# An MLP made of seven products: its operands' sums taken product by product, its weights' sums moved to VectorE, and its products in another order

## The chip, the cores and the metric

The kernel runs on one core of a Trainium2 chip. The metric is the device time of one execution in microseconds (us). Before the change it is 1749.95 us, the median of three runs (1748.13 to 1752.63). Engines are named as in the profile: PE is TensorE, DVE VectorE, ACT ScalarE, POOL GpSimd and SP SyncE.

## The reference

An encoder of two layers goes over 768 tokens (512 of one batch, 256 of the other) with 1024 features. Layer 0 mixes neighbourhood and grouped-query attention, layer 1 is differential attention. Behind each attention stands an MLP, which is what the change touches:

```python
h = rmsnorm(x, ln_mlp[layer])
x = x + jnp.square(jax.nn.relu(h @ w_up[layer])) @ w_down[layer]   # 1024 -> 4096 -> 1024
```

After layer 1 comes a last RMSNorm. Everything is in float32.

## The kernel before

**Products.** Activations stay transposed: features on the 128 partitions, tokens along the row. Each float32 operand is split into a high part, which ACT writes (whi, th, c), and the rest, which DVE subtracts (wlo, and the second half of th and c); a product is then three matmuls: high by high, high by low, low by high. In the MLP both matrix products are cut into 2 by 2 blocks (the tokens into halves A and B of 384) and made of seven block products instead of eight, so there are sums of blocks to make before the products and sums of products after them.

**The up projection** goes over 16 slices of 256 hidden features (mp). `weights()` makes four sums of weight blocks on POOL (L839) and splits them. The sums of activation blocks are made once per layer. `first()` splits the four plain blocks (c 0 to 3) while the output projection of the attention is still running. `second()` makes the other four (c 4 to 7): for each of four feature rows j it makes one scaled copy on ACT (L803) and four sums on DVE (L790), and splits four results with `put` (ACT and DVE, L116 and L117). The first slice is made of the eight plain products, which need c 0 to 3 only; `second()` runs beside it. The second slice takes its products in the order 1, 3, 2, 6, 4, 7, 5, so c 6 is the first sum that PE needs. The tile t of `second()` has three buffers, shared with z, in which a slice's results stand. `finish` (L873 on) writes a slice's squared results and their sums to DRAM, in seven slots: three by a DMA on ACT's queue straight from z, four by two DMAs on POOL's queue after more DVE sums.

**The down projection** has 28 steps: seven products n, each over four quarters i of the hidden features. A step is 48 matmuls (four output blocks r, four slices q, three parts). Before it, `operand` loads the slot from DRAM (tr, L915, SP's queue) and splits it (th); `fetch` loads two weight tiles (L986, SP's queue, three steps ahead); `sums` adds them on POOL to the tile kept from the product before (L993, for products 5, 6, 3 and 7, two per step); `halves` splits the sum (L80, L81). In the loop the order is: fetch of step s+3, sums and operand of s+2, halves of s+1, then the matmuls of s (L1034). At the end of a product its four PSUM banks are folded into the accumulators e, f and h or into x (L862, L1007); products 1 and 7 end with a longer run of such operations.

Tile sets the semaphores and the order on each engine, starting from the order of the program. What the PE is to do next waits in order; a DVE instruction that waits holds up the ones behind it, and so does a DMA in SP's queue.

Of the kernel before, what the change touches and what calls it, by code (L numbers as in the profile page):

```python
# [11 lines left out]
F32 = mybir.dt.float32  # L12
F32R = mybir.dt.float32r
AF = mybir.ActivationFunctionType
ALU = mybir.AluOpType
# [22 lines left out]
def kernel(ctx: ExitStack, tc: tile.TileContext, a: dict, y: bass.AP):  # L38
# [90 lines left out]
    def gcol(g, k):  # L129
        return gains[:, g, k : k + 1]  # L130
# [643 lines left out]
    def mlp(layer, src, o, x, es):  # L774
# [10 lines left out]
        def put(pool, c, j, src, gain=None):  # L785
            t = comb[c, j] = pool.tile([P, 2, HT], F32R, tag=f"c{c}", name=f"c{c}", bufs=4)
            halve(t[:, 0], t[:, 1], src, gain)

        def stt(out, x_, s, y_, op):
            nc.vector.scalar_tensor_tensor(out=out, in0=x_, scalar=s, in1=y_, op0=ALU.mult, op1=op)  # L790
# [5 lines left out]

        def second():

            ts = []
            for j in range(4):  # L800
                xa, xb = x[j], x[j + 4]
                t = up.tile([P, 4, HT], F32, tag="z", name="t", bufs=3)
                nc.scalar.activation(t[:, 0], xa[:, A], AF.Copy, scale=gcol(g, j))  # L803
                stt(t[:, 1], xa[:, B], gcol(g, j), t[:, 0], ALU.subtract)
                stt(t[:, 2], xb[:, A], gcol(5 + layer, j + 4), t[:, 1], ALU.subtract)
                put(g2, 6, j, t[:, 2])
                stt(t[:, 3], xb[:, B], gcol(g, j + 4), t[:, 2], ALU.add)
                put(g2, 4, j, t[:, 3])
                stt(t[:, 0], xb[:, A], gcol(g, j + 4), t[:, 0], ALU.subtract)
                put(g2, 7, j, t[:, 0])  # L810
                put(g2, 5, j, t[:, 1])

        run(out_proj(src, o, None, x, 1, first))
        es.close()
# [46 lines left out]
        def add(out, x_, y_, op=ALU.add):  # L861
            nc.vector.tensor_tensor(out=out, in0=x_, in1=y_, op=op)  # L862
# [49 lines left out]
        def operand(n, i):  # L912

            tr = pa_.tile([P, ND, HT], F32, tag="tr", name="tr", bufs=2)
            nc.sync.dma_start(tr, T[i][:, SLOT[n]])  # L915
            th = pa_.tile([P, 2, ND, HT], F32R, tag="th", name="th", bufs=3)
            halve(th[:, 0], th[:, 1], tr)
            return th

        for mp in range(first_mp, FF // 256):  # L920
            w = weights() if mp > first_mp else w2
            one = lambda n: product(bank(n), w[n], n)
            p1 = one(1)
            z = ztile()
            z12, z11, z22, z21 = z[:, 0, A], z[:, 0, B], z[:, 1, A], z[:, 1, B]
            nc.scalar.activation(z11, p1, AF.Copy)
            p3, p2 = one(3), one(2)
            if mp == FF // 256 - 1:

                g1s.close()  # L930
                pa_ = g1s.enter_context(tc.tile_pool(name=f"dna{layer}", bufs=4, reuse_waits="tile"))
                ths = [operand(4, 0)]
            add(z12, one(6), z11)
            add(z11, p2, z11)
            if wait:
                finish(wait.pop(0))
            p4 = one(4)
            add(z22, one(7), z12)
            add(z21, p4, z22, ALU.subtract)
            add(z12, p3, z12)  # L940
            if wait:
                finish(wait.pop(0))
            p5 = one(5)
            nc.vector.scalar_tensor_tensor(out=z22, in0=p5, scalar=-1.0, in1=z22, op0=ALU.mult, op1=ALU.subtract)
            add(z12, p5, z12)
            square(z)
            finish(z)
            if 4 <= mp < 4 + KD:
                nm.add(x[MO[mp - 4]])
            elif mp == 4 + KD:  # L950
                rt = nm.rstd()
# [10 lines left out]
        wds = ExitStack()  # L962
        ch = wds.enter_context(tc.tile_pool(name="ch", bufs=8, side="right", reuse_waits="tile"))
        wd = wds.enter_context(tc.tile_pool(name="wd", bufs=6, side="right", reuse_waits="tile"))
        e, f, h = (acs.tile([P, 4, HT], F32, name=f"{n}_{layer}") for n in "efh")
        PR = (0, 1)
        ORDER = (4, 5, 6, 3, 1, 7, 2)

        BLOCK = {1: 11, 2: 12, 7: 21, 4: 22, 5: 21, 6: 11, 3: 12}
        steps = [(n, i) for n in ORDER for i in range(NG)]  # L970
# [3 lines left out]
        def fetch(n, i):  # L974

            for rp in PR:
                off = (((layer * NG + i) * 4 + (11, 22, 21, 12).index(BLOCK[n])) * 2 + rp) * P * 1024
                if n in (1, 4) and (n, i) != (4, 0):
                    t = ch.tile([P, 1024], F32, tag="ch", name="ch", bufs=8)
                else:  # L980
                    third[0] += n != 4
                    if n == 4 or third[0] % 3 == 0:
                        t = wpool.tile([P, 1024], F32, tag="wraw", name="wd", bufs=3)
                    else:
                        t = wd.tile([P, 1024], F32, tag="wd", name="wd", bufs=6)
                nc.sync.dma_start(t, a["w_down"][off : off + P * 1024].rearrange("(p w) -> p w", w=1024))  # L986
                (kept if n in (1, 4) else new)[i, rp] = t

        def sums(n, i):
            for rp in PR:  # L990
                if n in (7, 5, 6, 3):
                    t = kept[i, rp]
                    nc.gpsimd.tensor_tensor(out=t, in0=t, in1=new.pop((i, rp)), op=ALU.add)  # L993

        def halves(n, i):
            for rp in PR:
                hi, lo = whilo(1024)
                wsplit(hi, lo, new.pop((i, rp)) if n == 2 else kept[i, rp])
                parts[n, i, rp] = hi, lo

        def fold(out, x_, op=ALU.add):
            add(out, out, x_, op)
# [4 lines left out]
            nc.vector.tensor_tensor(out=out, in0=x_, in1=rr, op=ALU.mult)  # L1007

        xb = lambda r, i, sl: x[2 * r + i][:, sl]
        for s in range(3):  # L1010
            fetch(*steps[s])
        halves(*steps[0])
# [2 lines left out]
        for s, (n, i) in enumerate(steps):  # L1015
            if s + 3 < len(steps):
                fetch(*steps[s + 3])
            if s + 2 < len(steps):
                sums(*steps[s + 2])
                ths.append(operand(*steps[s + 2]))  # L1020
            if s + 1 < len(steps):
                halves(*steps[s + 1])
            if i == 0:
                odd = ORDER.index(n) % 2
                banks = [ps_tile("at" if odd or r == 3 else "mm", "dn")[:, :HT] for r in range(4)]
            th = ths.pop(0)

            for passes in (((0, 0), (1, 0)), ((0, 1),)) if s == 0 else (((0, 0), (0, 1), (1, 0)),):
                for r, ps in enumerate(banks):
                    w = parts[n, i, r // 2]  # L1030
                    for q in range(ND):
                        c = (r % 2) * 512 + q * P
                        for a_, b_ in passes:
                            nc.tensor.matmul(ps, w[a_][:, c : c + P], th[:, b_, q], start=i + q + a_ + b_ == 0,  # L1034
                                             stop=i == NG - 1 and q == ND - 1 and a_ == 1)
            if i == NG - 1:
                for r, ps in enumerate(banks):
                    if n == 4:
                        nc.scalar.activation(f[:, r], ps, AF.Copy)
                    if n == 5:  # L1040
                        nc.scalar.activation(h[:, r], ps, AF.Copy)
                    if n == 3:
                        add(e[:, r], ps, h[:, r])
                    if n in (6, 1, 7):
                        fold(f[:, r], ps, ALU.subtract)
                        fold(h[:, r], ps)
                    if n == 1:
                        fold(e[:, r], ps)
                    if n in (1, 2):
                        t = acs.tile([P, HT], F32, tag="t", name="t", bufs=4)  # L1050
                        scaled(t, ps, B)
                        fold(xb(r, 0, B), t)
                if n == 1:
                    scaled(e, e, A)
                    for r in range(4):
                        fold(xb(r, 0, A), e[:, r])
                if n == 7:
                    scaled(h, h, A)
                    for r in range(4):
                        fold(xb(r, 1, A), h[:, r], ALU.subtract)  # L1060
                    scaled(f, f, B)
                    for r in range(4):
                        fold(xb(r, 1, B), f[:, r])
            if layer == 1 and n == 2 and i < NG - 1:
                last[0](i)
            elif layer == 1 and n == 7 and i == NG - 1:
                tiles = iter([(e, r) for r in range(4)] * 4)

                def sq():
                    e_, r = next(tiles)  # L1070
                    return e_[:, r]

                last = [final(x, sq, s_, R2[:, A]) for s_ in (0, HT)]
        if layer == 1:
# [208 lines left out]
```

## Time and profile before

| | |
|---|---|
| median of three runs | 1749.95 us |
| the profiled execution: its time | 1750.86 us |
| its span | 1749.1 us |
| PE busy | 1708.8 us (98%) |
| DVE busy | 1356.3 us (78%) |
| ACT busy | 874.0 us (50%) |
| POOL busy | 568.7 us (33%) |

The profile is one execution. A busy PE means that a matmul was in it, at whatever clock was granted. In a timeline the number in square brackets is the idle time of the engine just before the instruction, and after the arrow stands what ended it. A matmul of the MLP is 128x384 and starts every 175 ns when nothing holds it up.

### The profile page before, as it was taken

The page shows a single profiled execution, that of the slowest core. Times are in us where ns is not written, and L with a number is a line of the kernel's source. Part 1 is how long each engine was busy: PE and PEld are TensorE (multiplying, and loading weights), DVE is VectorE, ACT ScalarE, POOL GpSimd, SP SyncE. Part 2 cuts the span into 40 slices and gives each one's busy share as a digit, 9 for nine tenths or more (in the row PEclk, how much of TensorE's full clock was granted, in tenths as well). Part 3 has the DMA queues.
Part 4 walks back from the last instruction along what each step waited for, and adds up shares of the span by engine and source line. Part 5 has one row for each costly group of instructions (what it writes and reads, how often), then busy time and mean ns, then how long its engine had stood idle before and what let it go on. Part 6 is the DMA issues. An engine that isn't in the chain of part 4 may idle for free. (4 is left out here: it accounts for less than half of the span.)

```text
span 1749.1 us, 28353 instructions
## 1 busy us (share of the span) xinstructions
PE 1708.8 (98%) x10964; PEld 1623.4 (93%) x10964; DVE 1356.3 (78%) x2214; ACT 874.0 (50%) x1553; POOL 568.7 (33%) x443
## 2 busy tenths in 40 slices
PE   8999999999999999999999999999999999999997
PEld 7888888889999999999999999988899999899997
DVE  7888647499777699888676776776898776899885
ACT  6765434365444453444435555554555444544442
POOL 2200000025555288340021222210346553693501
PEclk9999999999999999999999999999999999999998
DMA  4111222414544687853410110122145546868521
GB/s 170 37 46 49 69 77 91 136 47 147 178 165 156 224 300 258 301 163 133 130 53 25 49 49 22 55 64 92 48 154 170 167 167 198 293 241 326 188 73 72
DMA packets 74597, 235.42 MB, mean 135 GB/s; under 512 B 7904, under 2 KB 25056, under 8 KB 74464
## 3 DMA queue, kind: packets, MB, share of 16 engines
q1 hardware_dynamic: 52480, 186.93, 32.1%
q0 software_dynamic: 7168, 25.17, 4.0%
q10 hardware_dynamic: 14816, 21.52, 3.4%
q8 instruction: 86, 1.41, 0.3%
q14 instruction: 47, 0.39, 0.1%
HBM read 182.47 MB, written 50.33 MB: 133 GB/s over the span
## 5 line engine op out<-in xcount | busy, mean ns | idle before, releaser
L854 PE MATMUL up<-c,whi 128*128 128x384 f32 x1808 | 463.8, 338 | 5.4 <-ACT c L116 4.3
L1034 PE MATMUL dn<-th,whi 128*128 128x384 f32 x1792 | 461.6, 339 | 3.7 <-DVE th L117 3.7
L854 PEld LDWEIGHTS up<-c,whi 128*128 128x128 f32 x1808 | 328.1, 188 | 7.4 <-ACT c L116 5.0
L1034 PEld LDWEIGHTS dn<-th,whi 128*128 128x128 f32 x1792 | 326.6, 188 | 4.6 <-DVE th L117 4.2
L1034 PE MATMUL dn<-th,wlo 128*128 128x384 f32 x896 | 302.9, 339 | 5.9 <-DVE wlo L81 5.9
L854 PE MATMUL up<-c,wlo 128*128 128x384 f32 x904 | 304.1, 338 | 0.5 <-DVE wlo L81 0.5
L839 POOL TENSOR_TENSOR s<-wraw 128x512 f32<-128x512 f32 x60 | 92.8, 1553 | 412.5 <-PE npv L601 258.9
L993 POOL TENSOR_TENSOR ch<-ch,wd 128x1024 f32<-128x1024 f32 x52 | 174.7, 3375 | 86.3 <-DVE wlo L81 76.0
L81 DVE TENSOR_TENSOR wlo<-ch,whi 128x1024 fp32r<-128x1024 f32 x80 | 157.8, 1998 | 27.0 <-ACT whi L80 26.8
L1034 PEld LDWEIGHTS dn<-th,wlo 128*128 128x128 f32 x896 | 168.7, 188 | 7.5 <-DVE wlo L81 7.5
L854 PEld LDWEIGHTS up<-c,wlo 128*128 128x128 f32 x904 | 170.2, 188 | 1.2 <-DVE wlo L81 1.2
L80 ACT ACTIVATE whi<-wraw 128x1024 fp32r<-128x1024 f32 (+3 forms) x128 | 116.3, 910 | 92.8 <-PE up L854 57.0
L81 DVE TENSOR_TENSOR wlo<-wraw,whi 128x1024 fp32r<-128x1024 f32 (+3 forms) x132 | 145.6, 1103 | 17.4 <-ACT whi L80 16.7
L80 ACT ACTIVATE whi<-ch 128x1024 fp32r<-128x1024 f32 x80 | 84.6, 1062 | 132.7 <-PE dn L1034 94.2
L117 DVE TENSOR_TENSOR th<-tr,th 128x1536 fp32r<-128x1536 f32 x56 | 143.7, 2566 | 5.8 <-ACT th L116 5.6
L80 ACT ACTIVATE whi<-s 128x1024 fp32r<-128x1024 f32 x60 | 63.8, 1064 | 118.6 <-PE up L854 106.8
L196 PE MATMUL dqk<-whi,xh 128*128 128x256 f32 x384 | 114.7, 299 | 0.0
L81 DVE TENSOR_TENSOR wlo<-s,whi 128x1024 fp32r<-128x1024 f32 x60 | 83.4, 1390 | 35.3 <-ACT whi L80 35.2
L116 ACT ACTIVATE th<-tr 128x1536 fp32r<-128x1536 f32 x56 | 83.0, 1482 | 49.6 <-DMA tr<-T 45.3
L196 PE MATMUL dqk<-whi,xl 128*128 128x256 f32 x384 | 107.5, 280 | 0.0
L196 PE MATMUL dqk<-wlo,xh 128*128 128x256 f32 x384 | 107.2, 279 | 0.0
L706 ACT ACTIVATE de<-ds,m 128x512 f32<-128x512 f32 (+1 forms) x96 | 58.3, 612 | 81.6 <-DVE m L704 81.6
(231 smaller groups left out, 3773.4 us busy)
## 6 DMA issues: line engine op xcount, KB each, us to landing
wd<-in_w_down_dram SPq DMA_DIRECT2D x84, 512.0 KB, 5.2
tr<-T SPq DMA_DIRECT2D x56, 768.0 KB, 5.2
wraw<-in_w_up_dram SPq DMA_DIRECT2D x64, 512.0 KB, 3.7
T<-t POOLq DMA_DIRECT2D x64, 384.0 KB, 3.2
T<-z ACTq DMA_DIRECT2D x32, 576.0 KB, 3.0
ch<-in_w_down_dram SPq DMA_DIRECT2D x28, 512.0 KB, 6.1
wraw<-in_w_in_o_dram SPq DMA_DIRECT2D x24, 512.0 KB, 3.6
wraw<-in_w_in_e_dram SPq DMA_DIRECT2D x16, 512.0 KB, 3.7
```

The lines of the kernel that those rows point to most:

```text
L80: nc.scalar.activation(hi, raw, AF.Copy)
L81: nc.vector.tensor_tensor(out=lo, in0=raw, in1=hi.bitcast(F32), op=ALU.subtract)
L116: nc.scalar.activation(hi, src, AF.Copy)
L117: nc.vector.tensor_tensor(out=lo, in0=src, in1=hi.bitcast(F32), op=ALU.subtract)
L196: nc.tensor.matmul(ps[:, :256], st[:, tk], col(k, part, 0, 256), start=(k == 0 and i == 0), stop=(k == KD - 1 and i == 2))
L706: nc.scalar.activation(e, s, AF.Exp, bias=m, scale=1.0, accum_out=l2[:, c : c + 1])
L839: nc.gpsimd.tensor_tensor(out=d_, in0=x_, in1=y_, op=ALU.add)
L854: nc.tensor.matmul(ps, part[a_][:, base + k * P : base + (k + 1) * P], t[:, b_], start=start and k + i == 0, stop=stop and k == 3 and i == 2)
L993: nc.gpsimd.tensor_tensor(out=t, in0=t, in1=new.pop((i, rp)), op=ALU.add)
L1034: nc.tensor.matmul(ps, w[a_][:, c : c + P], th[:, b_, q], start=i + q + a_ + b_ == 0, stop=i == NG - 1 and q == ND - 1 and a_ == 1)
```

## The change

`second()` gets room for all four rows at once (two z buffers, the ninth x tile, and the tile R) and goes over the rows once per product: c 6 of all rows, then c 4, then c 7, then c 5. In the down projection the weight sums go from POOL to DVE (`fold` instead of `nc.gpsimd.tensor_tensor`), the products come in the order 1, 7, 4, 5, 6, 3, 2, halves of s+1 now stand ahead of operand and sums of s+2, and the accumulators are combined by `settle`, which puts pieces in a list of which each later step takes one. A fourth accumulator u takes the place of the tile t. The last norm's squares go to u instead of e.

```diff
         def second():
-            ts = []
-            for j in range(4):
+            za, zb = (up.tile([P, 4, HT], F32, tag="z", name="t", bufs=3) for _ in range(2))
+            xt = xo_tile("t").rearrange("p (a t) -> p a t", a=2)
+            rt_ = cpool.tile([P, NT], F32, tag="R", name="t", bufs=1).rearrange("p (a t) -> p a t", a=2)
+            ts = ((za[:, 0], za[:, 1], za[:, 2]), (zb[:, 0], zb[:, 1], zb[:, 2]),
+                  (za[:, 3], zb[:, 3], xt[:, 0]), (xt[:, 1], rt_[:, 0], rt_[:, 1]))
+            for j, (t0, t1, t2) in enumerate(ts):
                 xa, xb = x[j], x[j + 4]
...
-                stt(t[:, 3], xb[:, B], gcol(g, j + 4), t[:, 2], ALU.add)
-                put(g2, 4, j, t[:, 3])
...
+                nc.scalar.activation(t0, xa[:, A], AF.Copy, scale=gcol(g, j))
+                stt(t1, xa[:, B], gcol(g, j), t0, ALU.subtract)
+                stt(t2, xb[:, A], gcol(5 + layer, j + 4), t1, ALU.subtract)
+                put(g2, 6, j, t2)
+            for j, (t0, t1, t2) in enumerate(ts):
+                stt(t2, x[j + 4][:, B], gcol(g, j + 4), t2, ALU.add)
+                put(g2, 4, j, t2)
+            for j, (t0, t1, t2) in enumerate(ts):
+                stt(t0, x[j + 4][:, A], gcol(g, j + 4), t0, ALU.subtract)
+                put(g2, 7, j, t0)
+            for j, (t0, t1, t2) in enumerate(ts):
+                put(g2, 5, j, t1)
...
-        ORDER = (4, 5, 6, 3, 1, 7, 2)
+        ORDER = (1, 7, 4, 5, 6, 3, 2)
...
-                    nc.gpsimd.tensor_tensor(out=t, in0=t, in1=new.pop((i, rp)), op=ALU.add)
+                    fold(t, new.pop((i, rp)))
...
+        def settle(n):
+            if n == 1:
+                due.append(lambda: quarter(0, B, e))
+            if n == 6:
+                due.append(lambda: (fold(f, u, ALU.subtract), scaled(f, f, B)))
+                due.append(lambda: (quarter(1, B, f), fold(e, u)))
+                due.append(lambda: (fold(h, u), scaled(h, h, A)))
+                due.append(lambda: quarter(1, A, h, ALU.subtract))
+            if n == 3:
+                due.append(lambda: (scaled(e, e, A), quarter(0, A, e)))
...
-            if s + 2 < len(steps):
-                sums(*steps[s + 2])
-                ths.append(operand(*steps[s + 2]))
             if s + 1 < len(steps):
                 halves(*steps[s + 1])
+            if s + 2 < len(steps):
+                ths.append(operand(*steps[s + 2]))
+                sums(*steps[s + 2])
+            if due:
+                due.pop(0)()
```

`quarter` folds four 128x384 blocks into x. At the end of a product ACT now copies the banks of 1 (to u), 7 (to h) and 5 (to e); DVE folds or scales those of 1, 4, 5, 6, 3 and 2.

## Rows read from the trace of the kernel before

**Rows 1.** The page's head and busy times: us, share of the span, instructions.
```profile
span 1749.1 us, 28353 instructions
PE 1708.8 (98%) x10964; PEld 1623.4 (93%) x10964; DVE 1356.3 (78%) x2214; ACT 874.0 (50%) x1553; POOL 568.7 (33%) x443
```

**Rows 2.** Waits of PE: who waited for whom, us in total, times, longest us.
```profile
PE dn L1034 <- DVE wlo L81: 5.9, 5, 1.8
```

**Rows 3.** Timeline of PE, matmuls behind an idle time: start, us, instruction, [idle <- by].
```profile
390.58 0.44 PE L854 MATMUL up<-c,whi 128*128 128x384 f32 x1 [2.19 <-ACT c L116]
391.55 0.69 PE L854 MATMUL up<-c,whi 128*128 128x384 f32 x1 [0.53 <-DVE c L117]
...
1268.79 0.45 PE L854 MATMUL up<-c,whi 128*128 128x384 f32 x1 [2.15 <-ACT c L116]
...
1299.28 0.44 PE L854 MATMUL up<-c,wlo 128*128 128x384 f32 x1 [0.53 <-DVE wlo L81]
...
1507.01 0.53 PE L1034 MATMUL dn<-th,whi 128*128 128x384 f32 x1 [3.37 <-DVE th L117]
...
1672.99 0.44 PE L1034 MATMUL dn<-th,wlo 128*128 128x384 f32 x1 [1.31 <-DVE wlo L81]
```

**Rows 4.** Windows: length, busy us (x) by engine, granted PE clock, DMA share, GB/s.
```profile
375.00:398.00 23.00, 20.29 (x107) 19.71 (x106) 22.36 (x36) 15.70 (x29) 5.95 (x4) 0.93 0.17 63
...
1276.00:1300.00 24.00, 23.47 (x133) 22.90 (x132) 22.96 (x29) 12.92 (x15) 17.14 (x11) 1.00 0.51 162
1503.00:1511.00 8.00, 4.61 (x17) 4.18 (x16) 7.82 (x3) 3.53 (x4) 8.00 (x3) 0.79 0.84 302
...
715.00:760.00 45.00, 45.00 (x257) 45.00 (x257) 35.74 (x30) 19.03 (x16) 14.07 (x6) 1.00 0.78 268
```

**Rows 5.** Groups of DVE, then POOL, 625 to 715 us: count, busy us, mean ns.
```profile
L117 DVE TENSOR_TENSOR th<-tr,th 128x1536 fp32r<-128x1536 f32 x11 | 39.3, 3573 | 2.0 <-ACT th L116 2.0
L81 DVE TENSOR_TENSOR wlo<-ch,whi 128x1024 fp32r<-128x1024 f32 x14 | 35.0, 2531 | 1.4 <-ACT whi L80 1.4
...
L993 POOL TENSOR_TENSOR ch<-ch,wd 128x1024 f32<-128x1024 f32 x17 | 61.3, 3630 | 5.0 <-DVE wlo L81 4.7 <-DMA wd<-in_w_down_dram 0.4
```

**Rows 6.** Groups of DVE, 800 to 840 us, where POOL does nothing.
```profile
L81 DVE TENSOR_TENSOR wlo<-wd,whi 128x1024 fp32r<-128x1024 f32 x8 | 9.6, 1218 | 5.0 <-ACT whi L80 5.0
L117 DVE TENSOR_TENSOR th<-tr,th 128x1536 fp32r<-128x1536 f32 x4 | 7.0, 1751 | 0.2 <-ACT th L116 0.2
```

**Rows 7.** Groups of DVE, 1253.9 to 1276 us, then one of 1276 to 1299.3.
```profile
L790 DVE SCALAR_TENSOR_TENSOR t<-x,gains,t 128x384 f32<-128x384 f32 x16 | 12.0, 800 | 0.0
L117 DVE TENSOR_TENSOR c<-t,c 128x384 fp32r<-128x384 f32 x16 | 8.0, 550 | 0.0
...
L152 DVE TENSOR_TENSOR acc<-acc,sq 128x768 f32<-128x768 f32 x3 | 5.1, 1688 | 0.0
```

**Rows 8.** Waits of DVE: all of 1253.9 to 1299.3 us, then all of 398 to 436.
```profile
DVE t L862 <- ACT z L871: 1.0, 1, 1.0
...
DVE z L862 <- PE up L854: 0.7, 1, 0.7
DVE t L862 <- ACT z L871: 0.5, 1, 0.5
```

**Rows 9.** Start of the second down projection: ACT, DVE and POOL in the timeline.
```profile
1501.66 1.49 ACT L116 ACTIVATE th<-tr 128x1536 fp32r<-128x1536 f32 x1 [5.83 <-DMA tr<-T]
...
1503.18 3.77 DVE L117 TENSOR_TENSOR th<-tr,th 128x1536 fp32r<-128x1536 f32 x1 [3.21 <-ACT th L116]
...
1502.98 6.21 POOL L993 TENSOR_TENSOR wd<-wd 128x1024 f32<-128x1024 f32 x2 [5.22 <-DMA wd<-in_w_down_dram]
...
1523.29 6.50 POOL L993 TENSOR_TENSOR ch<-ch,wd 128x1024 f32<-128x1024 f32 x2 [3.53 <-DMA wd<-in_w_down_dram]
```

**Rows 10.** DMA in 1480 to 1503 us: load, then an issue with us to landing.
```profile
DMA packets 2132, 7.03 MB, mean 306 GB/s; under 512 B 218, under 2 KB 703, under 8 KB 2131
...
T<-z ACTq DMA_DIRECT2D x1, 576.0 KB, 12.3
```

More of the change, by code (lines that the diff above doesn't have):

```diff
@@ L797, in second @@
         def second():
-            ts = []
-            for j in range(4):
-                xa, xb = x[j], x[j + 4]
[L802 to L806, printed above, removed]
-                stt(t[:, 3], xb[:, B], gcol(g, j + 4), t[:, 2], ALU.add)
-                put(g2, 4, j, t[:, 3])
-                stt(t[:, 0], xb[:, A], gcol(g, j + 4), t[:, 0], ALU.subtract)
-                put(g2, 7, j, t[:, 0])
-                put(g2, 5, j, t[:, 1])
+            za, zb = (up.tile([P, 4, HT], F32, tag="z", name="t", bufs=3) for _ in range(2))
[4 more added lines that the diff above has]
+            for j, (t0, t1, t2) in enumerate(ts):
+                xa, xb = x[j], x[j + 4]
+                nc.scalar.activation(t0, xa[:, A], AF.Copy, scale=gcol(g, j))
[10 more added lines that the diff above has]
+                put(g2, 5, j, t1)
         run(out_proj(src, o, None, x, 1, first))
@@ L931, in mlp @@
                 pa_ = g1s.enter_context(tc.tile_pool(name=f"dna{layer}", bufs=4, reuse_waits="tile"))
-                ths = [operand(4, 0)]
+                ths = [operand(1, 0)]
             add(z12, one(6), z11)
@@ L964, in mlp @@
         wd = wds.enter_context(tc.tile_pool(name="wd", bufs=6, side="right", reuse_waits="tile"))
-        e, f, h = (acs.tile([P, 4, HT], F32, name=f"{n}_{layer}") for n in "efh")
+        e, f, h, u = (acs.tile([P, 4, HT], F32, name=f"{n}_{layer}") for n in "efhu")
         PR = (0, 1)
-        ORDER = (4, 5, 6, 3, 1, 7, 2)
+        ORDER = (1, 7, 4, 5, 6, 3, 2)
         BLOCK = {1: 11, 2: 12, 7: 21, 4: 22, 5: 21, 6: 11, 3: 12}
@@ L977, in fetch @@
                 off = (((layer * NG + i) * 4 + (11, 22, 21, 12).index(BLOCK[n])) * 2 + rp) * P * 1024
-                if n in (1, 4) and (n, i) != (4, 0):
+                if n in (1, 4) and (n, i) != (1, 0):
                     t = ch.tile([P, 1024], F32, tag="ch", name="ch", bufs=8)
                 else:
-                    third[0] += n != 4
-                    if n == 4 or third[0] % 3 == 0:
+                    third[0] += n != 1
+                    if n == 1 or third[0] % 3 == 0:
                         t = wpool.tile([P, 1024], F32, tag="wraw", name="wd", bufs=3)
@@ L1009, in mlp, with quarter @@
         xb = lambda r, i, sl: x[2 * r + i][:, sl]
+        due = []
+        def quarter(i, sl, t, op=ALU.add):
+            for r in range(4):
+                fold(xb(r, i, sl), t[:, r], op)
+        def settle(n):
[8 more added lines that the diff above has]
+                due.append(lambda: (scaled(e, e, A), quarter(0, A, e)))
         for s in range(3):
@@ L1037, in mlp @@
                 for r, ps in enumerate(banks):
+                    if n == 1:
+                        nc.scalar.activation(u[:, r], ps, AF.Copy)
+                        scaled(e[:, r], ps, B)
+                    if n == 7:
+                        nc.scalar.activation(h[:, r], ps, AF.Copy)
                     if n == 4:
-                        nc.scalar.activation(f[:, r], ps, AF.Copy)
+                        add(f[:, r], ps, h[:, r], ALU.subtract)
                     if n == 5:
-                        nc.scalar.activation(h[:, r], ps, AF.Copy)
+                        nc.scalar.activation(e[:, r], ps, AF.Copy)
+                        fold(h[:, r], ps)
@@ L1042, in mlp @@
+                    if n == 6:
+                        fold(u[:, r], ps)
                     if n == 3:
[L1043 to L1047, printed above, removed]
-                        fold(e[:, r], ps)
[L1049 to L1063, printed above, removed]
+                        fold(e[:, r], ps)
@@ L1064, in mlp @@
+                    if n == 2:
+                        scaled(f[:, r], ps, B)
+                        fold(xb(r, 0, B), f[:, r])
+                settle(n)
             if layer == 1 and n == 2 and i < NG - 1:
                 last[0](i)
-            elif layer == 1 and n == 7 and i == NG - 1:
-                tiles = iter([(e, r) for r in range(4)] * 4)
+            elif layer == 1 and n == 3 and i == NG - 1:
+                tiles = iter([u[:, r] for r in range(4)] * 4)
                 def sq():
-                    e_, r = next(tiles)
-                    return e_[:, r]
+                    return next(tiles)
```

## The prediction

> **What bounds the kernel now.** I read the page's head first: PE is busy for 1708.8 of 1749.1 us [rows 1], so the kernel is a row of matmuls with some 40 us of holes in it, and no other engine's busy time counts unless it makes a hole. So the next view is who PE waits for. In the down projections it waits five times for a wlo, 5.9 us in all, the longest 1.8 [rows 2], and twice for a th, 3.37 [rows 3] and 0.29; DVE makes both. The timeline then places each hole. By stage:
>
> - `second()`, layer 0: 2.19 and 0.53 us for c [rows 3]. The granted clock of the window around it is 0.93: TensorE fell to its lower level, 1.2 GHz, behind these holes, which costs (1 - 0.93) x 23 = 1.6 us more [rows 4]. Together 4.3.
> - `second()`, layer 1: 2.15 and 0.52 for c, and 0.53 for a wlo 30 us later [rows 3]. Together 3.2. The clock doesn't fall.
> - Down projection, layer 0: three of the five holes for wlo, 1.17, 1.84 and 1.31. Together 4.3.
> - Down projection, layer 1: 3.37 and 0.29 for th, 1.31 (shown) and 0.29 for wlo [rows 3]: 5.3. The window at the 3.37 has a granted clock of 0.79, which is (1 - 0.79) x 8 = 1.7 us more [rows 4]. Together 7.0.
>
> That is 18.8 us, and the change can't win much more: the other holes lie in the attentions, at the start and in the last norm, which stay as they are. A matmul starts every 45.00 / 257 = 175 ns where nothing waits [rows 4], so a step of 48 is 8.4 us, before and after.
>
> The last view is what makes DVE late. Between 625 and 715 us POOL makes the weight sums, 3.63 us each, and in that stretch DVE takes 3.57 us for a th and 2.53 for a wlo [rows 5]. Where POOL does nothing the same instructions take 1.75 and 1.22 [rows 6].
>
> **Weight sums on DVE.** In a step of 8.4 us DVE makes one th and two wlo: before, 3.57 + 2 x 2.53 = 8.6 us [rows 5], more than the step has. After the change POOL is idle there: 1.75 + 2 x 1.22 = 4.2 us [rows 6], and two sums come on top. A DVE sum of 128x1024 is not in the trace. The nearest row is wlo, the same shape with two operands in SBUF: 1.22 us, and 2.53 beside POOL [rows 5, 6]; these are the ends. I take 1.22, since nothing of POOL is left beside it: 4.2 + 2.4 = 6.6 us of 8.4. DVE gets a fifth of a step of slack where it had none, so the 1.17 and 1.84 of layer 0 and the two 0.29 of layer 1 go, 3.6 us. At 2.53 a step with sums would need 9.3, in 16 of a layer's 28 steps, and I would count half of the 3.6.
>
> What now stands behind the sums on DVE: they are issued ahead of the next step's wlo and th, so a weight tile that lands late would hold those up, where it held only POOL before. The cover is that weights are fetched three steps, 25 us, ahead.
>
> **The order of products, settled in pieces.** The two holes of 1.31, one per layer, follow the end of product 1, where DVE runs 20 operations of 128x384 in one go, 0.55 us each (as the c of [rows 7]), then a scaling and four more: some 15 us. After the change no product ends with more than eight such operations, and the pieces of `settle` come one to a step. The heaviest steps are the first two of product 3: 6.6 and 3.5 to 3.9 us of pieces (two operations of 1536 columns at 1.75 [rows 6], or four of 0.55 and one of 1.75), 1.7 to 2.1 over the step each. A burst of 15 us made a hole of 1.3, so I cost an excess of 3.8, spread over two steps, at nothing. Both holes go, 2.6 us; at the other end both stay.
>
> **The start of the second down projection.** The 3.37 hole is a chain: ACT stands 5.83 us for the third step's operand, takes 1.49 for its high part, and DVE 3.77 for the rest, because POOL started a sum at 1502.98 [rows 9]. Without that sum it is 1.75 [rows 6]: 2.0 of the 3.37 goes and about 1.35 stays, since the load itself is late. The clock fell behind 3.37 and behind 2.19 and 0.53, and did not behind 2.15 and 0.52 [rows 3, 4]; 1.35 is below all of them, so the 1.7 goes too. 3.7 us; ends 2.0, if the clock still falls, and 5.1, if the load comes sooner. The new first product reads slot 0, written straight from z by ACT's queue, and one could hope that its operands come sooner. But the DMA engines move 306 GB/s in this stretch and the last write of z takes 12.3 us to land [rows 10]. I count nothing for it.
>
> The Trainium skill (Trainium Kernel Development and Optimization, section Key Constraints) says that DMAs issued from SP, ACT and POOL all run on the same 16 DMA engines and interleave. By that another slot by another queue brings nothing, and the 12.3 us agree; who takes ACT's queue for a path of its own would add the 1.35.
>
> Down projections together: 3.6 + 2.6 + 3.7 = 9.9.
>
> **`second()` product by product.** DVE makes 16 sums and 16 splits in either order, 12.0 + 8.0 us busy [rows 7]; nothing is removed. But c 6 of the last row, which PE needs first, comes behind 12 operations instead of 27, and rows 2 and 3 no longer wait for a buffer, so the holes at c go. Then DVE is the limit: from 1253.9 to 1299.3 it waits once, 1.0 us [rows 8], and at 1299.28 PE again waits for it, 0.53 us for a wlo [rows 3]. PE comes to that matmul earlier by what it no longer waits, DVE by 1.0 at most. So in layer 1 the stall moves there and 1.0 of 3.2 is won. In layer 0 PE had lost 1.6 more to the clock and met no hole at this place: 1.6 - 0.53 = 1.1 of room, plus 1.2 of waits that DVE can give up [rows 8], 2.3 of 4.3. Ends: nothing; and 3.2 and 4.3, if the norm's accumulations, 5.1 us in the way of that wlo [rows 7] with nobody waiting for them, are put behind it.
>
> A price of the new buffers: the first z and the two tiles of `second()` fill the three z buffers, so the second slice's first result waits for a tile that is read last by c 5. The bank that holds it is needed again a slice later, so I cost it at nothing; without that cover it is up to the four splits of c 5, 2.2 us per layer [rows 7].
>
> **Sum.** 9.9 + 2.3 + 1.0 = 13.2 us off the profiled execution's 1750.86 (its span of 1749.1 and 1.8 around it): 1737.7. That execution is 0.9 above the median of 1749.95, so by the median it is 1736.8. I say 1737.
>
> **Rivals.**
>
> - *All holes go.* The accumulations move behind the weights and the load comes in time. For it: those 5.1 us can wait. Against: it was Tile that put them there, and it still sets the order. 18.8 us: 1731.
> - *Half of the gain.* `second()` gives nothing (-3.3), the clock still falls at the start (-1.7), and a sum costs 2.53 (-1.8): 13.2 - 6.8 = 6.4, 1743.5; with the 2.2 for the buffers in one layer 1745.7.
> - *Nothing on balance.* As above in both layers, and the two holes behind product 1 stay: 13.2 - 6.8 - 4.4 - 2.6, no gain: 1750.
> - *Slower: the sums wait for weights at the head of DVE's queue.* Where the sums begin POOL stood 5.22 and 3.53 us for weight tiles [rows 9]. On DVE such waits stop th and wlo behind them. It decides from the point where a wait exceeds DVE's slack, 1.8 us a step. Price: 8.7 in each layer, 17.4, and a fall of the clock at each, 1.7 x 2: 20.8 - 13.2 = 7.6 slower, 1757.5. Against it: the operand's load stands between the fetches in SP's queue and needs th done to have a buffer, and th is faster now; and the tile that POOL waited for had landed by 1502.98, when the new order's first sums begin.
>
> **Chances.** Forecast (9 to 16 won) 0.55; all holes 0.18; half 0.16; nothing 0.05; slower 0.06. A measurement of this kernel can tell 0.3% from no change, 5.2 us. Two thirds of the half case lie beyond that: faster 0.55 + 0.18 + 0.10 = 0.83, the same 0.06 + 0.05 = 0.11, slower 0.06. The range goes from all holes gone, 1730.5, to the half case with the buffers, 1745.5; outside are the last two and the edges of the first two.
>
> **What would show it.** In the down projections: no sums on POOL, th at 1.75 and wlo at 1.22 throughout, the new sums at 1.2, and no wait of PE but one of 1.4 us near the start of layer 1, without a fall of the clock. In `second()`: no wait of PE for c, and some 30 us later a longer one for wlo, in layer 1 above all. I am wrong if DVE waits for weight loads, if PE still waits for c, or if the wait behind `second()` doesn't grow.

## The result and the profile after

The changed kernel takes **1737.01 us** (median of 4 runs, 1734.63 to 1738.23) beside 1749.38 for the kernel before (4 runs): ratio 0.9925 [0.9907, 0.9942]. The forecast was 1737. The total is right, but, as will be seen, not all the terms under it are.

The head and the busy times of the kernel after, which answer to [rows 1]; the profiled run took 1737.35 us, 13.5 less than that of the kernel before:

```profile
span 1735.5 us, 28286 instructions
PE 1704.4 (98%) x10964; PEld 1619.8 (93%) x10964; DVE 1316.8 (76%) x2252; ACT 875.5 (50%) x1561; POOL 353.1 (20%) x379
```

POOL lost 215.6 us of busy time, and DVE, which took over the sums, is 39.5 us *less* busy than before. The groups of DVE from 625 to 715 us say why; they answer to [rows 5, 6]:

```profile
L81 DVE TENSOR_TENSOR wlo<-ch,whi 128x1024 fp32r<-128x1024 f32 x20 | 24.5, 1223 | 14.2 <-ACT whi L80 12.1 <-DMA tr<-T 1.7
L868 DVE TENSOR_TENSOR ch<-ch,wd 128x1024 f32<-128x1024 f32 x18 | 21.9, 1222 | 0.4
L117 DVE TENSOR_TENSOR th<-tr,th 128x1536 fp32r<-128x1536 f32 x12 | 21.0, 1751 | 2.3 <-ACT th L116 2.3
```

The new sum takes 1.222 us, a wlo 1.223 instead of 2.531, a th 1.751 instead of 3.573. In this stretch DVE now waits 12.1 us for ACT's whi, where it waited 1.4 before [rows 5]: it has room.

Waits of PE after (who waited for whom: us in total, times, longest); they answer to [rows 2]:

```profile
PE up L860 <- DVE wlo L81: 4.5, 6, 1.1
...
PE dn L1060 <- DVE th L117: 1.3, 1, 1.3
...
PE dn L1060 <- ACT th L116: 0.5, 1, 0.5
```

And the timeline of PE after, matmuls behind an idle time, which answers to [rows 3]:

```profile
398.39 0.45 PE L860 MATMUL up<-c,wlo 128*128 128x384 f32 x1 [1.09 <-DVE wlo L81]
...
411.84 0.44 PE L860 MATMUL up<-c,wlo 128*128 128x384 f32 x1 [0.61 <-DVE wlo L81]
...
414.77 0.44 PE L860 MATMUL up<-c,wlo 128*128 128x384 f32 x1 [0.56 <-DVE wlo L81]
...
1496.00 0.45 PE L1060 MATMUL dn<-th,whi 128*128 128x384 f32 x1 [0.49 <-ACT th L116]
...
1497.80 0.44 PE L1060 MATMUL dn<-th,whi 128*128 128x384 f32 x1 [1.35 <-DVE th L117]
```

No hole for c is left, and none for a wlo in a down projection. What is left is three holes for wlo behind `second()` in each layer (those of layer 1, 1.09, 0.58 and 0.55, are of the same size), and 0.49 and 1.35 at the start of the second down projection.

**Where the 13.5 us went.** PE's timeline cuts both executions into stages, from first matmul to first matmul; a down projection ends with the start of its last one (us):

| stage | before | after | won |
|---|---|---|---|
| to the first matmul of up, layer 0 | 363.9 | 362.5 | 1.4 |
| up, with `second()`, layer 0 | 244.7 | 244.0 | 0.7 |
| down, layer 0 | 241.4 | 236.4 | 5.0 |
| to up, layer 1 | 392.2 | 391.8 | 0.4 |
| up, with `second()`, layer 1 | 243.9 | 243.7 | 0.2 |
| down, layer 1 | 247.3 | 243.0 | 4.2 |
| last norm and output | 15.8 | 14.1 | 1.6 |

The last column is worked out before rounding. The change is in four of these rows, and there it won 10.1. The other 3.4 come from places that are the same in both kernels but for the tile that takes the last norm's squares, and the clock tells most of it. Windows of before, then after, with the start and the end in each (length, busy us (x) by engine, granted clock, DMA share, GB/s):

```profile
0.00:50.00 50.00, 41.60 (x316) 40.26 (x316) 38.96 (x120) 35.03 (x84) 13.50 (x28) 0.97 0.43 148
...
1733.33:1749.10 15.77, 4.64 (x20) 3.85 (x19) 4.58 (x10) 1.32 (x3) 3.75 (x4) 0.58 0.27 100
```
```profile
0.00:50.00 50.00, 41.59 (x322) 39.83 (x322) 40.01 (x124) 36.42 (x89) 14.20 (x30) 1.00 0.44 148
...
375.00:398.00 23.00, 22.12 (x125) 21.30 (x123) 23.00 (x41) 16.37 (x29) 4.38 (x4) 1.00 0.20 76
...
1495.00:1503.00 8.00, 6.16 (x25) 5.57 (x25) 7.02 (x6) 4.33 (x4) 0.00 (x0) 0.79 1.00 375
...
1721.41:1735.50 14.09, 3.14 (x20) 2.35 (x19) 4.59 (x10) 1.33 (x3) 3.74 (x4) 0.70 0.30 112
```

At the start the clock fell in the execution of before, (1 - 0.97) x 50 = 1.5 us, and not in that of after, though nothing differs there. Of the twelve kernels below, six show that fall and six don't. So it is chance, worth about 1.5 us either way in any one profiled execution. In the last norm the clock falls in both, earlier in that of before: the same 20 matmuls take 4.64 us there and 3.14 after, another 1.5. This stage, too, varies by itself: in the twelve kernels below it lies between the 14.1 of after and the 15.8 of before. In layer 0 it doesn't fall behind `second()` any more (0.93 in [rows 4]), but it still falls at the start of the second down projection: 0.79, as in [rows 4].

### The profile page after: what moved, and what is told of

The parts are those of the page before. It is cut to its first block, busy times and chain, and to the rows that moved or that the text cites. A ratio compares the mean times of both kernels' runs of the same rounds, so it can differ in the third digit from the quotient of the medians.

```text
span 1735.5 us, 28286 instructions
## 1 busy us (share of the span) xinstructions
PE 1704.4 (98%) x10964; PEld 1619.8 (93%) x10964; DVE 1316.8 (76%) x2252; ACT 875.5 (50%) x1561; POOL 353.1 (20%) x379
## 5 line engine op out<-in xcount | busy, mean ns | idle before, releaser
L80 ACT ACTIVATE whi<-ch 128x1024 fp32r<-128x1024 f32 x88 | 93.3, 1064 | 172.9 <-PE dn L1060 161.3
L845 POOL TENSOR_TENSOR s<-wraw 128x512 f32<-128x512 f32 x60 | 86.6, 1448 | 424.2 <-PE npv L601 258.8
L81 DVE TENSOR_TENSOR wlo<-ch,whi 128x1024 fp32r<-128x1024 f32 x88 | 107.1, 1222 | 54.6 <-ACT whi L80 49.7
L167 POOL TENSOR_TENSOR rt<-ms,nhalf 128x6 f32<-128x6 f32 (+1 forms) x6 | 8.9, 1482 | 503.7 <-DVE ms L166 503.7
L117 DVE TENSOR_TENSOR th<-tr,th 128x1536 fp32r<-128x1536 f32 x56 | 98.1, 1752 | 7.6 <-ACT th L116 7.3
L868 DVE TENSOR_TENSOR z<-up,z 128x384 f32<-128x384 f32 x180 | 96.4, 549 | 0.9
```

Of the source, the lines that this page charges most:

```text
L80: nc.scalar.activation(hi, raw, AF.Copy)
L81: nc.vector.tensor_tensor(out=lo, in0=raw, in1=hi.bitcast(F32), op=ALU.subtract)
L117: nc.vector.tensor_tensor(out=lo, in0=src, in1=hi.bitcast(F32), op=ALU.subtract)
L167: nc.gpsimd.tensor_tensor(out=rt, in0=ms, in1=nhalf[:, :n], op=ALU.pow)
L845: nc.gpsimd.tensor_tensor(out=d_, in0=x_, in1=y_, op=ALU.add)
```

## The experiments

Each ratio is to the kernel before on the same chip, with its 95% interval. All kernels compute the whole reference.

### The two halves of the change

`e1_down_only`: the kernel after with the old `second()`. `e2_second_only`: the kernel before with the new `second()`.

The loops go back as a whole; only their heads are shown:

```diff
-            for j, (t0, t1, t2) in enumerate(ts):    # e1: after's second(), product by product
+            for j in range(4):                       # before's, row by row; e2 the other way round
```

> The new down projections with the old second(). My theory (DVE is full behind second(), so its new order wins little): the holes at c come back, 2.2 and 0.5 us in each layer, but the holes for wlo some 15 to 30 us later (2.2 us in all per layer in the changed kernel) go or shrink to 0.5; the down projections stay without holes but for the start of layer 1's. About 1 to 2 us over the changed kernel, 1738 to 1739. Rival (each hole at c is worth what it measures, 5.4 us and the clock's 1.6): 1742 to 1744.

> Only the new second(), the old down projections. My theory: no hole at c, holes for wlo behind it of about 2.3 us in each layer, 1 to 2 us faster than before, 1747.5 to 1748.5; the down projections keep their 4.3 and 7.0 us. Rival (the holes at c are worth what they measure): 5 to 7 us faster, 1742 to 1744.

Measured: e1 **1737.2** (0.9931 [0.9916, 0.9946]), e2 **1748.5** (0.9992 [0.9982, 1.0001]). The down projections are the gain; `second()` alone can't be told from nothing. e1's timeline has the holes at c back:

```profile
388.86 0.44 PE L854 MATMUL up<-c,whi 128*128 128x384 f32 x1 [2.25 <-ACT c L116]
...
419.34 0.45 PE L854 MATMUL up<-c,wlo 128*128 128x384 f32 x1 [0.53 <-DVE wlo L81]
```

and its windows over the two `second()` show the clock falling in the other layer than before:

```profile
375.00:398.00 23.00, 20.22 (x114) 19.49 (x113) 23.00 (x41) 17.07 (x29) 4.43 (x4) 1.00 0.16 59
1253.00:1276.00 23.00, 20.32 (x105) 19.50 (x104) 22.08 (x40) 14.74 (x24) 1.98 (x3) 0.93 0.24 83
```

So behind holes of 2.2 and 0.5 us the clock sometimes fell and sometimes did not. Over all traces it fell in six of the ten stretches with the old `second()` (before, e1, e4, e11 and e14, two layers each) and in none of the eighteen with the new one. That is also all that the new order can be seen to win. Cut as in the table, the up projection takes 243.9 to 244.0 us with the old `second()` where the clock doesn't fall and 243.7 to 244.2 with the new one (after, e2, e3, e5, e8, e10); where it falls, 244.5 to 245.0. The holes only moved. Waits of PE in e2:

```profile
PE dn L1040 <- DVE wlo L81: 7.8, 6, 1.9
PE up L860 <- DVE wlo L81: 4.7, 7, 1.1
```

The old holes at c, some 5.4 us in two layers, became 4.7 us for wlo. The down projections of e2 have the code of before, and yet there is no hole at the start of the second one, where before has 3.37; more on this below.

### Which part of the down projection's change does it

`e3_sums_on_pool`: the kernel after, the weight sums back on POOL. `e4_sums_only`: the kernel before, the sums on DVE and nothing else.

```diff
-                    fold(t, new.pop((i, rp)))
+                    nc.gpsimd.tensor_tensor(out=t, in0=t, in1=new.pop((i, rp)), op=ALU.add)
```
```diff
-                    nc.gpsimd.tensor_tensor(out=t, in0=t, in1=new.pop((i, rp)), op=ALU.add)
+                    nc.vector.tensor_tensor(out=t, in0=t, in1=new.pop((i, rp)), op=ALU.add)
```

> The changed kernel with the weight sums back on POOL, order and pieces as changed. My theory (POOL's sums slow DVE's th and wlo): th back at about 3.6 us and wlo at 2.5 in the stretches with sums, holes of PE for wlo and th again, 3 to 5 us in each layer, 1743 to 1747. Rival (the order of the products and the pieces made the gain): th and wlo slow, but holes under 1 us in all, 1737 to 1739.

> The kernel before with one line changed: the weight sums on DVE. My theory: th and wlo at 1.75 and 1.22 everywhere, the holes of 1.17, 1.84 and 0.29 us go, the 3.37 becomes about 1.4. But the run of 20 operations at the end of product 1 is still there and now the sums of product 7 stand in the same queue: its hole stays at 1.3 us or grows to as much as 3.7 in each layer. 1741 to 1747. Rival (the sums alone are the change; the pieces are worth nothing once POOL is idle): no hole at the end of product 1, 1739 to 1741.

Measured: e3 **1737.04** (0.9937 [0.9916, 0.9957]), e4 **1740.36** (0.9945 [0.9928, 0.9961]). Here my theory fell: with the sums on POOL, the rest of the change wins as much. e3's only wait of its down projections for a wlo:

```profile
PE dn L1060 <- DVE wlo L81: 0.7, 1, 0.7
```

e3's groups of DVE from 685 to 790 us show that it is still slowed, if less than before, and its windows that it has just enough room (a stretch in which PE makes product 7 and the steps of product 4, which need no sums, are prepared, then one full of sums):

```profile
L81 DVE TENSOR_TENSOR wlo<-ch,whi 128x1024 fp32r<-128x1024 f32 x25 | 53.8, 2162 | 4.0 <-ACT whi L80 3.9
...
L117 DVE TENSOR_TENSOR th<-tr,th 128x1536 fp32r<-128x1536 f32 x13 | 36.9, 2842 | 0.4 <-ACT th L116 0.2
```
```profile
645.00:680.00 35.00, 35.00 (x199) 34.71 (x199) 28.03 (x22) 16.66 (x17) 10.80 (x5) 1.00 0.84 317
690.00:760.00 70.00, 70.00 (x400) 70.00 (x399) 67.44 (x33) 30.33 (x29) 51.81 (x17) 1.00 0.64 217
```

DVE is busy for 67.44 of 70 us beside POOL's sums, and PE has not one hole. In e4, which keeps the old order, the holes of 1.17, 1.84 and 0.29 are gone, 0.6 is left of the 3.37, and the holes behind product 1 are as they were:

```profile
PE dn L1034 <- DVE wlo L81: 2.6, 2, 1.3
...
PE dn L1034 <- DVE th L117: 0.6, 1, 0.6
```

So sums on DVE and the rest of the change are two remedies for the same 3.6 us; either alone takes all or nearly all of it away. With the sums on POOL it is a close fit, though: of e3's four executions three took 1735.5 to 1737.4 us and one 1743.4, and the profiled one is the fastest.

### What the 1.31 holes are, and whether the pieces matter

`e5_settle_at_once`: the kernel after, each product's pieces all at its end. `e11_halves_first`: the kernel before with the loop's new order only. `e14_two_lines`: e11 and e4 together.

```diff
                 settle(n)
+                while due:
+                    due.pop(0)()
```
```diff
-            if s + 2 < len(steps):
-                sums(*steps[s + 2])
-                ths.append(operand(*steps[s + 2]))
             if s + 1 < len(steps):
                 halves(*steps[s + 1])
+            if s + 2 < len(steps):
+                ths.append(operand(*steps[s + 2]))
+                sums(*steps[s + 2])
```

> The changed kernel with the pieces of settle all at the end of their product. Theory A (sums spread by the new order and a free DVE are enough): behind product 6 DVE runs some 15 us of pieces in one go, PE waits for nothing, 1736 to 1738. Theory B, of the prediction (the pieces are what removes the hole behind the long run): a hole of 1.0 to 1.5 us for wlo behind product 6 in each layer, 1738 to 1741.

> The kernel before with one edit of the change: halves of step s+1 stand ahead of sums and operand of s+2. Theory A (the hole of 1.31 us behind product 1 is a th of 1.75 us that stands ahead of the wlo PE needs): both holes of 1.31 go, the others of the down projections stay, 2 to 3 us faster than before, 1747. Theory B (the long run itself is the hole): they stay within 0.3 us, 1749 to 1750.

> The kernel before with two edits only: sums on DVE, and halves of s+1 ahead of sums and operand of s+2; old order of products, no pieces, old second(). Theory A (these two remove all holes of the down projections): no hole there but for the start of layer 1's, as fast as the changed kernel within 1.5 us, 1736 to 1739. Theory B (the order or the pieces are needed too): a hole stays behind product 1, 1740 or more.

Measured: e5 **1736.14** (0.9913 [0.9897, 0.993]), without a hole in a down projection, though behind product 6 of layer 0 DVE runs its pieces in one go, with one wlo between them (777.38 to 790.7 us); e11 **1745.82** (0.9974 [0.9964, 0.9985]); e14 **1737.45** (0.9929 [0.9908, 0.995]). The timeline of DVE at the end of product 1, in the kernel before:

```profile
1668.18 1.95 DVE L862 TENSOR_TENSOR x<-x,e 128x384 f32<-128x384 f32 x4
1670.06 1.75 DVE L117 TENSOR_TENSOR th<-tr,th 128x1536 fp32r<-128x1536 f32 x1
1671.72 2.35 DVE L81 TENSOR_TENSOR wlo<-ch,whi 128x1024 fp32r<-128x1024 f32 x2
```

and in e11:

```profile
1668.56 1.96 DVE L862 TENSOR_TENSOR x<-x,e 128x384 f32<-128x384 f32 x4
1670.44 2.36 DVE L81 TENSOR_TENSOR wlo<-ch,whi 128x1024 fp32r<-128x1024 f32 x2
1672.71 1.76 DVE L117 TENSOR_TENSOR th<-tr,th 128x1536 fp32r<-128x1536 f32 x1
```

The burst is the same in both. What turned it into a hole of 1.31 is the th of 1.75 us behind it, which is for the step after next and stood ahead of the wlo that PE needed next. Three lines put wlo first, and both of these holes are gone. The waits that e11 has left in the down projections aren't the old ones, though:

```profile
PE dn L1034 <- DVE wlo L81: 4.7, 4, 1.9
PE dn L1034 <- DVE th L117: 4.1, 3, 1.9
```

That is 8.8 us in seven holes, against 9.6 in seven before. In layer 0 the holes came down from 4.3 to 3.3, but in layer 1 there are a th of 1.90 and a wlo of 1.85 where before had 0.29 for each, 5.5 in all against 5.3. So in this execution, the slowest of e11's eight, the loop's order alone mostly moved the waits of a DVE that POOL slows. With the sums on DVE besides (e14), the kernel before is as fast as the whole change, and PE waits 0.2 us in the down projections.

`e10_pool_at_once`: e3 and e5 together, to see where the pieces could still matter.

```diff
-                    fold(t, new.pop((i, rp)))
+                    nc.gpsimd.tensor_tensor(out=t, in0=t, in1=new.pop((i, rp)), op=ALU.add)
...
+                while due:
+                    due.pop(0)()
```

> The changed kernel with the weight sums on POOL and the pieces of settle at once, so that of the down projection's edits only the order of products and halves first are left. Theory A (the order is a remedy of its own: product 4 without sums after 7 lets DVE catch up): no hole over 1 us in the down projections, 1737 to 1739. Theory B (with a slowed DVE the pieces matter): holes of 1 to 3 us behind product 6 in each layer, 1740 to 1744.

Measured: **1740.05** (0.9941 [0.9921, 0.9961]). Waits of PE:

```profile
PE dn L1060 <- DVE th L117: 2.2, 2, 1.4
PE dn L1060 <- DVE wlo L81: 1.2, 1, 1.2
```

Three holes, 3.3 us, where e3 has one of 0.7, but the pieces don't make them. Two stand in product 1 (1.43 at 635.2 us, 0.73 at 1500.5), before any piece is due. The third, 1.16 at 1527.7, has e3's 0.72 for a counterpart, and DVE runs the same operations in the same order ahead of both, in e3 and then in e10:

```profile
1515.24 2.18 DVE L868 TENSOR_TENSOR x<-x,e 128x384 f32<-128x384 f32 x1
1517.34 3.96 DVE L117 TENSOR_TENSOR th<-tr,th 128x1536 fp32r<-128x1536 f32 x1
```
```profile
1519.97 2.19 DVE L868 TENSOR_TENSOR x<-x,e 128x384 f32<-128x384 f32 x1
1522.08 3.96 DVE L117 TENSOR_TENSOR th<-tr,th 128x1536 fp32r<-128x1536 f32 x1
```

Behind product 6, where the longest list of pieces is settled, e10 runs it at once and has no hole. So no run shows a use for the pieces, neither theory placed the holes, and the times of e3 and e10 aren't apart by their intervals.

### What is left behind `second()` and at the start

`e7_norm_later`: the kernel after, where the norm's accumulations may be issued only behind their slice's last combination. `e8_operand_early`: the kernel after, where the third step's operand is loaded ahead of the weights of steps 2 and 3 instead of behind them.

```diff
-            nc.vector.scalar_tensor_tensor(out=z22, in0=p5, ...)
+            mark = nc.vector.scalar_tensor_tensor(out=z22, in0=p5, ...)
...
-                nm.add(x[MO[mp - 4]])
+                with tc.issue_after(getattr(mark, "ins", mark)):
+                    nm.add(x[MO[mp - 4]])
```
```diff
...
-        for s in range(3):
+        for s in range(2):
             fetch(*steps[s])
         halves(*steps[0])
         ths.append(operand(*steps[1]))
+        ths.append(operand(*steps[2]))
+        with tc.issue_after(getattr(dma[-1], "ins", dma[-1])):
+            fetch(*steps[2])
...
-                ths.append(operand(*steps[s + 2]))
+                if s:
+                    ths.append(operand(*steps[s + 2]))
```

> The changed kernel with the accumulations of the MLP's norm held behind the slice in which the program has them (slices 4 to 11), so that they leave the stretch behind second(). My theory (DVE is the limit there, and what can wait stands in its way): the holes of 0.6 and 0.55 us for wlo some 15 us behind second() go in both layers, the first one of 1.1 stays, since no accumulation stands ahead of it: 2 to 2.5 us faster than the changed kernel, 1734 to 1736. Rival (POOL's sums set that stretch, whatever DVE does in it): the holes stay, 1737.

> The changed kernel with the load of the third step's operand ahead of the four weight tiles of the third and fourth step in SP's queue. My theory (this load is late because it stands behind six weight tiles at 300 GB/s): it lands in under 9 us instead of 14 at the start of layer 1's down projection, and th is never waited for there; worth 1.8 us and the fall of the clock, 1.7, where they occur, 1734 to 1737. Rival (the write of T shares the DMA engines and sets the landing): it still takes 12 us or more, and a hole of about 1 us stays in some executions, 1737.

Measured: e7 **1733.89** (0.9899 [0.9884, 0.9914]), e8 **1735.53** (0.991 [0.9895, 0.9924]). The timeline of DVE behind `second()` in the kernel after has accumulations between the weight halves, one of them stretched to 5.74 us:

```profile
397.13 1.21 DVE L81 TENSOR_TENSOR wlo<-wraw,whi 128x1024 fp32r<-128x1024 f32 x1
...
404.91 5.74 DVE L152 TENSOR_TENSOR acc<-acc,sq 128x768 f32<-128x768 f32 x1
410.57 1.21 DVE L81 TENSOR_TENSOR wlo<-wraw,whi 128x1024 fp32r<-128x1024 f32 x1
...
412.17 0.94 DVE L152 TENSOR_TENSOR acc<-acc,sq 128x768 f32<-128x768 f32 x1
```

In e7 they are gone from there, and of three holes per layer the first stays:

```profile
PE up L860 <- DVE wlo L81: 2.2, 2, 1.1
```

At the start of the second down projection the load in question is issued at 1480.1 us in the kernel after and at 1480.7 in e8. Its answers, after and e8:

```profile
DMA to landing us min/median/max: 14.3/14.3/14.3
```
```profile
DMA to landing us min/median/max: 4.2/4.2/4.2
```

In e8 no hole is left in either down projection. That hole also varies by itself, however: e3 and e5, which keep the late load, show none there, and e7 shows 0.35 and 1.35. So the one trace of e8 shows the load early, but not alone that this took the hole away. All fourteen traces together do. Here is, for each, the time of this load from issue to landing and the holes of PE for its th (us):

| kernel | landing | holes |
|---|---|---|
| after, e7 | 14.3, 14.3 | 1.84, 1.70 |
| before | 13.7 | 3.37, beside POOL's sum |
| e11, e10, e4 | 13.2, 12.9, 12.7 | 1.29, 0.73, 0.61 |
| e1, e14 | 12.2, 12.1 | none, 0.23 |
| e5, e3, e2 | 11.6, 11.4, 11.1 | none |
| e8, e12, e13 (load early) | 4.2, 4.2, 4.3 | none |

The hole follows the landing, and the landing varies where the stage's code is the same: by 2.7 us between after and e5, by 2.6 between before and e2.

`e12_both`: e7 and e8 together. `e13_finish_later`: e12, and the `finish` of the first slice, 128x768 sums of DVE that only feed the store to T, in the third slice instead of the second.

```diff
...
-        def finish(z):
-            mp = done.pop(0)
+        def finish(z, mp):
...
-            if wait:
-                finish(wait.pop(0))
+            if wait and mp > 1:
+                finish(*wait.pop(0))
```

> The changed kernel with the norm's accumulations held back and the third operand loaded early. My theory: behind second() only the hole of 1.1 us is left in each layer, the down projections have none: 3 to 4 us faster than the changed kernel, 1732 to 1734. Rival (they collide): the holes of 0.6 and 0.55 come back in one layer, 1735 or more.

> As the one before, and the sums that finish makes of the first slice (1.9 us of DVE) moved from the second slice into the third, behind its first product. My theory (the hole of 1.1 us is DVE's work ahead of a wlo): it shrinks to under 0.4 us in both layers, 1 to 1.5 us faster than the kernel with the two edits. Rival (ACT's high part sets it): it stays at 1.1.

Measured: e12 **1731.73** (0.9896 [0.9879, 0.9914]), e13 **1728.81** (1727.05 to 1730.11; 0.9879 [0.9861, 0.9897]). e13 is faster than the kernel before and than the change, whose interval begins at 0.9907. The timeline of DVE ahead of the wlo in question in the kernel after, then in e13:

```profile
392.07 0.54 DVE L868 TENSOR_TENSOR z<-up,z 128x384 f32<-128x384 f32 x1
392.54 0.94 DVE L868 TENSOR_TENSOR t<-z 128x768 f32<-128x768 f32 x1
...
393.87 0.54 DVE L790 SCALAR_TENSOR_TENSOR t<-t,z 128x384 f32<-128x384 f32 x1
```
```profile
393.63 0.54 DVE L868 TENSOR_TENSOR z<-up,z 128x384 f32<-128x384 f32 x1
394.10 1.21 DVE L81 TENSOR_TENSOR wlo<-wraw,whi 128x1024 fp32r<-128x1024 f32 x1
```

With the sums of t out of the way the first wlo starts at 394.10 instead of 397.13, and no matmul of the up or down projections waits for DVE any more; e13's busy times, of a span of 1727.4 us:

```profile
PE 1702.7 (99%) x10964; PEld 1620.7 (94%) x10964; DVE 1326.3 (77%) x2252; ACT 875.1 (51%) x1561; POOL 357.0 (21%) x379
```

## Why the prediction was right, and where it was not

- **Down projection, layer 0: 4.3 forecast, 5.0 measured.** All three holes went. The 0.7 on top is PE itself: 237.1 us busy there before, 236.4 after.
- **Down projection, layer 1: 5.6 forecast, 4.2 measured.** The two holes of 0.29 and that of 1.31 went, and of the 3.37 the 1.35 stayed that I had worked out, for a load that landed about as late as before (14.3 us, 13.7 before). The step that failed is "1.35 is below all of them, so the 1.7 goes too": ACT's high part of the same late load made a second hole of 0.49 just ahead, and behind these 1.84 us in two parts the clock fell as before, 0.79. A single hole's length compared with two others was no basis; nor had I asked how far the load's landing varies. It sets this hole, and the stage with it: 239.1 us in e5 and 239.3 in e1, where there is none, 242.9 in e7, beside the 243.0 here, and 244.8 in e2, whose down projections are those of before, beside 247.3.
- **`second()`: 3.3 forecast, 0.9 measured** (0.7 and 0.2 by stage). The mechanism was the one forecast: no wait for c, DVE the limit, and a longer wait for wlo behind. Its size was not: I let DVE give up its idle times and had PE's stall grow by the rest, but there are three holes per layer, 1.09, 0.61 and 0.56, where I counted one. The forecast priced the accumulations as an upside only; e7 takes two of the three holes away by moving them, and e13 the third by moving `finish`'s sums, which I hadn't named. By the other traces the 0.7 of layer 0 is the clock's fall, which before had there and the new `second()` nowhere; the holes gave nothing.
- **What made up for it: 3.4 us in stages that the change doesn't touch.** The term that I took from one execution, 1750.86, had its clock falls by chance. That the sum came out to 0.1 us is luck: by the stages that were changed it would have been 10.1 instead of 13.2, 1739.9. And the 10.1 is of this one pair: with e5's 239.1 in place of 243.0 it would be 14.0, with e2's 244.8 in place of 247.3 it would be 7.6. What the change wins on average is known no closer than by the interval of its ratio, 10 to 16 us.
- **Why the down projections gained, the forecast had right only in part.** That the weight sums on DVE win 3.6 is true in e4, but e3 shows that the rest of the change gives nearly the same without them. "A burst of 15 us made a hole of 1.3" is wrong as it stands: e11 keeps the burst and has no hole behind it, and e5 has the pieces at once and no hole. The order of halves and operand, three moved lines for which I had no term, is what took the 1.31 holes away. What makes room for POOL's sums in e3 isn't settled: e11 shows that the loop's order alone doesn't, and e10 has no hole that the pieces would have spared. That leaves the order of products, with the accumulators that go with it; no run tries it alone.
- **The rivals.** Of the three legs of "half of the gain" two came, or nearly: `second()` gave 0.9 of its 3.3, and the clock still fell at the start of the second down projection. The third, a sum at 2.53 us, did not: it takes 1.22. Slower, with sums waiting for weights, did not come: in the down projection of layer 0 DVE waits 0.7 us for a weight tile, in that of layer 1 not at all. "All holes go" is what e13 reaches with three more edits: 1728.8, against 1731 forecast for it.

## What to carry to other kernels

When an engine's queue holds work for the next step and for the one after, look which stands first: a 1.75 us operation one place too early made the hole for which a burst of 15 us was blamed. Before adding up remedies, ask whether two of them cure the same hole; their gains don't add. And split a difference of two executions by stage before crediting the change: here a quarter of it lay in stages that were the same, and one changed stage varies by 4 us with the landing of a load.

## What the runs showed of the hardware

- A DVE sum of 128x1024 takes 1.222 us, as a wlo of the same shape; in stretches with POOL's sums the wlo takes 2.16 (e3) to 2.53 us (before) on average, and the th of 1.75 takes 2.84 to 3.57.
- An accumulation that takes 0.94 us took 5.74 at 404.91 in the kernel after, while POOL was making sums of 128x512 and issuing two stores (401.89 to 409.8). In e7 a wlo stands in the same place and takes 5.28, from 407.18 to 412.46; there POOL had both stores issued by 407.54 and made three sums up to 411.4. Which of the two stretches it wasn't tried.
- The clock's falls aren't fixed by a stage's code: behind the same pair of holes, 2.2 and 0.5 us, it fell in layer 0 in the kernel before, in layer 1 in e1, e11 and e14, and in both in e4, and at the start in seven of fourteen profiled executions. Behind 0.49 and 1.35 us, less than 2 us apart, it fell (0.79); behind a single hole of 1.43 in e10 and behind 1.29 and 1.90, some 10 us apart, in e11 it stayed at 1.00.
- A load of the same tile (768 KB) lands 11.1 to 14.3 us after its issue behind the weight tiles, in eleven traces, and 4.2 to 4.3 ahead of them, in three.
